# Three moves of work between queues in a one-core transformer-layer kernel: the first block's transposes, two weight sums, and the order inside half of a product

## The chip, the core and the metric

The kernel runs on one core of a Trainium2 chip. The core has five engines with queues of their own, each working strictly in order: TensorE (PE, with its weight loads shown as PEld), VectorE (DVE), ScalarE (ACT), GpSimd (POOL) and SyncE (SP, which only issues DMAs here). The metric is device time in microseconds, the median of several runs of the whole program, 721.55 us before the change (721.35 to 722.12).

## What is computed

One layer on 512 positions of 1024 channels, all in float32, batch 1:

```
u = rms_norm(h, g_mix);  z = u @ w_in              # 1024 -> 4360 columns
y_a = sliding_window_attention(q_a, k_a, v_a, sinks) @ w_br_swa    # 8 heads of 64
y_b = forgetting_attention(q_b, k_b, v_b, f_b + b_forget) @ w_br_fox
h = h + (gates[:, :, 0] * y_a + gates[:, :, 1] * y_b) @ w_mix_out
u = rms_norm(h, g_mlp)
h = h + square(relu(u @ w_ff1)) @ w_ff2            # 1024 -> 4096 -> 1024
h = h + sigmoid(rms_norm(h, g_ple) @ w_ple_gate) * (p @ w_ple_proj)
out = rms_norm(h, g_final)
```

Float32 accuracy is kept on PE by writing each operand as a high half and a low half (`hi_lo`, L68: ACT casts the value to `fp32r`, DVE subtracts that from the value) and by summing three products: high by high, high by low, low by high.

## The kernel before, in words

**Order.** PE and POOL run in the order in which the program is written. In two stretches ACT and DVE do so too: in the whole start (L477, SP as well there) and from L1332 to the end of the third step of the feed-forward part (`man`, closed at L1382). Everywhere else the build lays out the order of ACT, DVE and SP on its own.

**The start (L477 to L544).** Four blocks of 128 positions are normalized and multiplied with the 648 columns of `w_in` that give the values and the forget logits. `square1` (L429) sums the squares of a block, one half on ACT and one on DVE; `scale1` (L443) has POOL turn the sum into the factor `rs` (two small operations in `rms_rstd`, L356: `n_ms`, then `n_rs`), and DVE scales both halves. `to_uT` (L373) transposes a half block on PE in four instructions and splits the result in high and low. `split_v(k)` (L451) splits one of eight slices of the weights: `wv_h` on ACT, `wv_l` on DVE. `v_mm(tb, k)` (L458) is six matmuls. For block 0 the written order is:

```
scale1(0, square1(0)); split_v(0)
to_uT half 0; v_mm(0, 0); split_v(1); v_mm(0, 1); split_v(2); split_v(3)
to_uT half 1; v_mm(0, 2); v_mm(0, 3)
acc = square1(1); split_v(4); split_v(5); scale1(1, acc); v_mm(0, 4); v_mm(0, 5)
```

Half 0 holds k = 0 to 3 of the block, half 1 holds 4 to 7.

**The feed-forward part (L1348 on).** Both big products are done in a scheme of seven block products in place of eight (Winograd's form of Strassen's): a product of pieces 1 to 7, of which 1 and 2 take a quadrant of the weights as it is, 3 a single quadrant too, and 5, 6, 7 and 4 take sums of quadrants. The hidden 4096 columns come in four quarters of two groups each. A quarter is 28 steps, written out in `STEPS` (L46): a and b are the first product (`f1`) of the quarter's two groups, A and B the second (`s2`):

```
a1 b1 a2 a5 b5 b2 a6 b6 a7 a3 b7 b3 A1 a4 b4 B1 A2 A5 B5 B2 A6 B6 A3 A7 B7 B3 A4 B4
```

Each step has one unit of weights. In the profile the units are numbered: the first quarter's a1 is u53, b1 u54, a2 u55, a5 u56, b5 u57, b2 u58, a6 u59, b6 u60, a7 u61, a3 u62, b7 u63, b3 u64, A1 u65, a4 u66, b4 u67, B1 u68, A2 u69, A5 u70, B5 u71. `emit_split` (L301) splits a unit (ACT L324, DVE L325, into one of four buffers). `sum_source` (L276) prepares the sum of quadrants ahead of that, in place, so a sum waits until the quadrant's earlier value has been split. The sums of A5, A7, B5 and B7 are done by DVE (L296); all others by an accumulating DMA that POOL issues (L298). The sums of b6 and b7 are emitted right after the split of b5 (`advance`, L328), inside the hand-ordered stretch. A quadrant's place takes the next load from memory (`emit_dma`, L246, issued by SP in order) once its last reader is done.

`win_mm` (L898) is the first product's step, 24 matmuls; `win_out` (L914) takes the result out of its bank (ACT L921 copies it, DVE L925 adds to it), and the next step in the same bank waits for that. `ff1_act` (L1257) applies relu and square on ACT; `ff2_op` (L1272) makes the operands 5, 6, 7 and 3 of the second product from sums of these, and splits them in `o` high (ACT L70) and `o` low (DVE L71).

`s2_mm` (L1296) is the second product's step: for each of two blocks of 128 positions six matmuls, with `oh`, `ol` the operand's halves and `wh`, `wl` the weights'. The order of the six is (j = 0: `oh wh`, `oh wl`, `ol wh`; then the same for j = 1).

Of the kernel before, what the change touches and what calls it, by code (L numbers as in the profile page):

```python
# [14 lines left out]
P = 128  # L15
# [35 lines left out]
def layer_kernel(ctx: ExitStack, tc: tile.TileContext, x, p, g_mix, w_in, b_forget, swa_sinks,  # L51
# [224 lines left out]
    def sum_source(i):  # L276

        if i in sources or i >= len(order) or not isinstance(order[i][1][0], (list, dict)):  # L280
            return
        emit_dma(i)
        key, (rs, pn, _), _ = order[i]

        first = {5: 1, 6: 5, 4: 6}.get(pn)
        if (first and unit_of[key[:-1] + (first,)] >= look["n"]
                or pn == 7 and unit_of[key[:-1] + (5,)] not in sources
                or any(raws[r]["tile"] is None for r in raws_of(i))):
            return
        if pn in (1, 2, 3):  # L290
            q = quadrant(i, pn in (2, 3), pn == 3)
        else:
            q = quadrant(i, 0, pn == 7)
            other = quadrant(i, *{5: (0, 1), 7: (1, 1), 6: (1, 1), 4: (1, 0)}[pn])
            if key[0] == "s2" and pn in (5, 7):
                nc.vector.tensor_tensor(q, q, other, ALU.add)  # L296
            else:
                nc.gpsimd.dma_start(q, other, accum_op=ALU.add)  # L298
        sources[i] = q if key[0] == "s2" else q.rearrange("q k (j c) -> q k j c", c=P)
# [70 lines left out]
                                           ALU.mult)  # L370
        return xn

    def to_uT(xn, uh, ul, tb, trp, name, tg="tr", halves=(0, 1)):  # L373

        for half in halves:
            tr = trp.tile([P, 4, P], F32, tag=tg, bufs=3, name=f"{name}_tr{half}")
            for j in range(4):
                k = half * 4 + j
                nc.tensor.transpose(tr[:, j, :], xn[:, k * P:(k + 1) * P], ident)
            sl = (slice(None), slice(half * 4, half * 4 + 4), slice(tb * P, (tb + 1) * P))  # L380
            hi_lo(uh[sl], ul[sl], tr)

    def new_uT(name):
        t = up.tile([P, 2 * KT * S + SHIFT], F32R, tag="u", bufs=1, name=name)
# [92 lines left out]
    with tc.manual_schedule(engines={ET.Activation, ET.DVE, ET.SP}):  # L477
        load_x(0)
        load_wv(0)
        load_wv(2)  # L480
        load_x(1)
        load_wv(4)
        load_wv(6)
        load_x(2)
        load_x(3)
        bcast_row(bf_bc, b_forget[0])
        bcast_row(sink_bc, swa_sinks[0])


        warm = psA.tile([P, 4, P], F32, tag="tr", bufs=3, name="warm")  # L490

        def warm_up(n):
            for j in range(n):
                nc.tensor.transpose(warm[:, j % 4, :], ident, ident)
        warm_up(N_WARM[0])
        ps = psA.tile([P, KT], F32, tag="mm", bufs=2, name="g_colps")
        nc.tensor.transpose(ps, g_row, ident[0:KT, 0:KT])
        nc.vector.tensor_copy(g_col, ps)
        warm_up(N_WARM[1])
        gps = []  # L500
        for half in range(2):
            ps = psA.tile([P, S], F32, tag="sc", bufs=3, name=f"g_ps{half}")
            for j in range(4):
                k = half * 4 + j
                nc.tensor.transpose(ps[:, j * P:(j + 1) * P],
                                    g_col[:, k:k + 1].to_broadcast([P, P]), ident)
            gps.append(ps)
        warm_up(N_WARM[2])
        scale1(0, square1(0))
        split_v(0)  # L510
        to_uT(xn1[0], uh, ul, 0, psA, "n1_0", halves=(0,))
        v_mm(0, 0)
        for k in (1, 2, 3):
            split_v(k)
            if k == 1:
                v_mm(0, 1)
        to_uT(xn1[0], uh, ul, 0, psA, "n1_0", halves=(1,))
        v_mm(0, 2)
        v_mm(0, 3)
        acc = square1(1)  # L520
        split_v(4)
        split_v(5)
        scale1(1, acc)
        v_mm(0, 4)
        v_mm(0, 5)
        split_v(6)
        split_v(7)
        for half in range(2):
            nc.scalar.copy(g_bc[:, half * 512:half * 512 + 512], gps[half])
        to_uT(xn1[1], uh, ul, 1, psA, "n1_1")  # L530
        v_mm(0, 6)
        v_mm(0, 7)
        for tb in range(1, NT):
            if tb < NT - 1:
                acc = square1(tb + 1)
                scale1(tb + 1, acc)
            v_out(tb - 1)
            for k in range(KT):
                v_mm(tb, k)
                if k == 4 and tb < NT - 1:  # L540
                    to_uT(xn1[tb + 1], uh, ul, tb + 1, psA, f"n1_{tb + 1}")
            if tb == 2:
                unit("ka")
        v_out(NT - 1)  # L544
# [751 lines left out]
    def s2_mm(g, pn):  # L1296
# [5 lines left out]
        for i in range(2):  # L1302
# [1 line left out]
                bank[g // 2, "2" + bk, i] = mm_tile(f"s2_{g}{bk}{i}", tg)  # L1304
            ps = bank[g // 2, "2" + bk, i]
            ts_ = slice(i * P, i * P + P)
            for j in range(2):
                for n, (o, w) in enumerate(((oh, wh), (oh, wl), (ol, wh))):
                    nc.tensor.matmul(ps, o[:, j, ts_], w[:, j, :],  # L1309
                                     start=tg != "" and j == 0 and n == 0,  # L1310
                                     stop=j == 1 and n == 2, skip_group_check=True)

    def s2_out(fq, pn):

# [178 lines left out]
```

## Time and profile before

| what | us |
|---|---|
| median of the runs | 721.55 |
| the profiled execution's own time | 721.84 |
| its span, first to last instruction | 720.1 |
| mean granted clock of TensorE | 0.997 |
| start until block 1 is transposed | about 17 |
| feed-forward part, four quarters of 28 steps | about 354 to 664 |

The span is what the profile's clock shows from the first to the last instruction; the program's own time has 1.7 us around it. PE is busy 98% of the span, so what matters is where it is not, and which instruction of which engine ended that idle time: in the rows of the profile this stands in square brackets, `[idle before <-releaser]`. An engine's gap that nobody waits for costs nothing.

### The profile page before, as it was taken

The numbers are of one execution on the slowest core, as the hardware profiler recorded it, in microseconds if no ns is written. First come the engines' busy times: TensorE is split into PE (matmuls) and PEld (weight loads), VectorE is DVE, ScalarE is ACT, GpSimd is POOL, SyncE is SP. The second block draws the span as 40 slices with busy tenths as digits, with TensorE's granted clock in tenths as the row PEclk, the third lists the DMA queues.
The fourth block names the chain that finished last, engine by engine and source line by source line (L and its number), as shares of the span: only waits on it lengthen the run. The fifth ranks groups of instructions, "written<-read, shape, count | busy, mean of one in ns | idle before, by whom it ended". The sixth has DMA issues, their size and how long they took to land.

```text
span 720.1 us, 11455 instructions
## 1 busy us (share of the span) xinstructions
PE 705.6 (98%) x4229; PEld 626.6 (87%) x4229; DVE 531.5 (74%) x900; ACT 449.4 (62%) x836; POOL 87.6 (12%) x127
## 2 busy tenths in 40 slices
PE   7999999999999999999999999999999999999995
PEld 6988888888888998888899789988999889988884
DVE  5567888877696556545879985899679966997564
ACT  5547888779863553344777646874578546866452
POOL 1011211100001200002410102010300020010101
PEclk9999999999999999999999999999999999999998
DMA  9256456670364894450995598739994689079002
GB/s 290 65 155 159 109 136 154 150 197 1 118 206 116 152 339 162 160 173 11 252 220 202 105 285 168 235 87 254 190 259 113 157 234 227 31 147 349 1 30 87
DMA packets 74055, 116.72 MB, mean 162 GB/s; under 512 B 6664, under 2 KB 44048, under 8 KB 74000
## 3 DMA queue, kind: packets, MB, share of 16 engines
q1 hardware_dynamic: 65792, 86.38, 37.9%
q0 software_dynamic: 8064, 29.36, 22.2%
q8 instruction: 33, 0.54, 0.3%
q10 hardware_dynamic: 144, 0.26, 0.1%
q14 instruction: 22, 0.18, 0.1%
HBM read 72.93 MB, written 4.19 MB: 107 GB/s over the span
## 4 chain that ended last, share of the span: by engine, by line
PE 85%; DVE 9%; ACT 2%; issue 2%; DMA 1%; POOL 0%; POOLq 0%; DVEq 0%; ACTq 0%
PE pf L74 5%; PE pf L76 5%; PE pf L75 5%; PE s_6x L1309 3%; PE s_4x L1309 3%; PE s_0x L1309 3%; PE s_2x L1309 3%; PE h_sc L752 2%; PE h_pv L822 2%; PE h_tr L810 2%; PE psy L75 2%; PE psy L76 2%; PE psy L74 2%; PE psm L76 2%; PE psm L75 2%; PE psm L74 2%
## 5 line engine op out<-in xcount | busy, mean ns | idle before, releaser
L298 POOL DMA_DIRECT2D wq<-wq x26 | 23.6, 942 | 174.9 <-DVE u154l L325 25.9
L770 ACT ACTIVATE s<-s,h_nm 128x128 f32<-128x128 f32 (+1 forms) x64 | 32.6, 512 | 5.9 <-DVE h_nm L763 5.1
L359 POOL TENSOR_SCALAR n_ms<-acc 128x1 f32<-128x1 f32 x15 | 6.3, 419 | 164.8 <-ACT junk L1075 100.4
L71 DVE TENSOR_TENSOR h_ptl<-h_tr,h_pth 128x512 fp32r<-128x512 f32 (+2 forms) x40 | 22.9, 604 | 3.9 <-ACT h_pth L70 3.6
L467 PE MATMUL va<-wv_h,u 128*128 128x320 f32 x64 | 20.1, 319 | 0.8 <-ACT u L70 0.7
L70 ACT CAST h_pth<-h_tr 128x512 fp32r<-128x512 f32 (+2 forms) x40 | 19.4, 523 | 1.8 <-PE h_tr L810 1.4
L70 ACT CAST u<-n_tr 128x512 fp32r<-128x512 f32 x22 | 12.2, 586 | 13.1 <-PE n_tr L1123 5.9
L810 PE MATMUL h_tr<-ident,s 128*128 128x128 f32 x136 | 19.6, 277 | 0.2
L467 PE MATMUL vb<-wv_h,u 128*128 128x328 f32 x64 | 19.6, 313 | 0.0
L298 POOL DMA_DIRECT2D wgw<-wgw x8 | 7.1, 970 | 101.9 <-DVE u25l L325 77.7
L71 DVE TENSOR_TENSOR u<-n_tr,u 128x512 fp32r<-128x512 f32 x22 | 14.6, 685 | 6.5 <-ACT u L70 6.5
L1075 ACT ACTIVATE junk<-h_sb 128x512 f32<-128x512 f32 x16 | 10.1, 630 | 12.3 <-DVE h_sb L1065 9.8
L822 PE MATMUL h_pv<-h_pth,v 128*128 128x256 f32 (+1 forms) x64 | 17.3, 291 | 0.0
L822 PE MATMUL h_pv<-h_ptl,v 128*128 128x256 f32 (+1 forms) x64 | 16.9, 305 | 0.3 <-DVE h_ptl L71 0.3
L810 PEld LDWEIGHTS h_tr<-ident,s 128*128 128x128 f32 x136 | 15.0, 141 | 2.0 <-ACT s L790 0.5
L1399 DVE TENSOR_TENSOR sgp<-sgp,pp 128x512 f32<-128x512 f32 (+1 forms) x9 | 5.7, 633 | 14.6 <-ACT sgp L1398 14.6
L1065 DVE TENSOR_TENSOR h_sb<-psm,h_sb 128x512 f32<-128x512 f32 x8 | 5.5, 689 | 14.3 <-PE psm L76 14.3
L790 ACT ACTIVATE s<-s,h_rec 128x128 f32<-128x128 f32 (+2 forms) x32 | 14.2, 482 | 2.3 <-DVE h_rec L784 2.3
L832 DVE TENSOR_TENSOR h_ao<-h_pv,h_ao 64x512 f32<-64x512 f32 x16 | 10.9, 681 | 6.1 <-ACT h_ao L831 5.8
L758 DVE CUSTOM_DVE_ANT_0 s<-h_sc,causal 128x128 f32<-128x128 f32 (+3 forms) x32 | 13.8, 482 | 0.3 <-PE h_sc L752 0.3
L784 DVE RECIPROCAL h_rec<-h_den 128x4 f32<-128x4 f32 x16 | 3.0, 185 | 14.5 <-ACT s L770 14.3
L822 PEld LDWEIGHTS h_pv<-h_ptl,v 128*128 128x128 f32 x64 | 12.1, 188 | 1.7 <-DVE h_ptl L71 0.8
(1607 smaller groups left out, 2773.8 us busy)
## 6 DMA issues: line engine op xcount, KB each, us to landing
wq<-in_w_ff_dram SPq DMA_DIRECT2D x45, 512.0 KB, 5.7
wq<-wq POOLq DMA_DIRECT2D x26, 512.0 KB, 5.1
wq_c<-in_w_ff_dram SPq DMA_DIRECT2D x9, 512.0 KB, 5.8
wg<-in_w_in_dram SPq DMA_DIRECT2D x4, 1024.0 KB, 5.4
wgw<-in_w_in_dram SPq DMA_DIRECT2D x8, 512.0 KB, 5.2
wgw<-wgw POOLq DMA_DIRECT2D x8, 512.0 KB, 5.8
wmix<-in_w_mix_out_dram SPq DMA_DIRECT2D x4, 1024.0 KB, 4.9
wpg<-in_w_ple_gate_dram SPq DMA_DIRECT2D x4, 1024.0 KB, 8.6
```

The source lines that it names most:

```text
L70: nc.scalar.copy(hi, src)
L71: nc.vector.tensor_tensor(lo, src, hi.bitcast(F32), ALU.subtract)
L74: nc.tensor.matmul(ps, lh, rh, start=start, stop=False)
L75: nc.tensor.matmul(ps, lh, rl, start=False, stop=False)
L76: nc.tensor.matmul(ps, ll, rh, start=False, stop=stop)
L298: nc.gpsimd.dma_start(q, other, accum_op=ALU.add)
L467: nc.tensor.matmul(ps, u[:, kk_, ts_], w[:, kk_, c0:c1], start=kk_ == 0 and n == 0, stop=kk_ == KT - 1 and n == 2)
L752: nc.tensor.matmul(ps[:, off:off + n], qs[i][z][:, qb * P:(qb + 1) * P], kk[i][z][:, k0:k0 + n], start=z == 0, stop=z == 1)
L770: nc.scalar.activation(sl, sl, AF.Exp, bias=nm[:, qb:qb + 1], accum_out=den[:, qb:qb + 1])
L810: nc.tensor.transpose(tr[:, n, :], c["s"][:, o, :], ident)
L822: nc.tensor.matmul(pv[:, q0:q0 + nq, :], V2[kb][:, c["v"], :], t[:, o:o + nq, :], start=n == 0, stop=n == 2 * NT - 1, skip_group_check=True)
L1309: nc.tensor.matmul(ps, o[:, j, ts_], w[:, j, :], start=tg != "" and j == 0 and n == 0, stop=j == 1 and n == 2, skip_group_check=True)
```

## The change

1. In the start, `to_uT` is cut in two: `to_uT_pe` (the four transposes of a half) and `to_uT_split` (its high and low half). For block 0 both halves' transposes are written ahead of everything else of PE, the second half's split comes behind `split_v(2)`, and `square1(1)` moves up from behind `v_mm(0, 3)` to ahead of `split_v(3)`. `v_mm(0, 1)` to `v_mm(0, 3)` keep their order on PE.
2. The sums of b6 and b7 of the first quarter (`("f1", 1, 6)` and `("f1", 1, 7)`, u60 and u63) are done by DVE in place of POOL's accumulating DMAs. The other three quarters keep the DMAs.
3. In `s2_mm` the six matmuls run as `oh wh`, `oh wl` for j = 0, the same for j = 1, then `ol wh` for j = 0 and for j = 1. This holds for all 56 steps of the second product.

```diff
-            if key[0] == "s2" and pn in (5, 7):
+            if key[0] == "s2" and pn in (5, 7) or key in (("f1", 1, 6), ("f1", 1, 7)):
                 nc.vector.tensor_tensor(q, q, other, ALU.add)
             else:
                 nc.gpsimd.dma_start(q, other, accum_op=ALU.add)
...
-    def to_uT(xn, uh, ul, tb, trp, name, tg="tr", halves=(0, 1)):
-
-        for half in halves:
-            tr = trp.tile([P, 4, P], F32, tag=tg, bufs=3, name=f"{name}_tr{half}")
-            for j in range(4):
-                k = half * 4 + j
-                nc.tensor.transpose(tr[:, j, :], xn[:, k * P:(k + 1) * P], ident)
-            sl = (slice(None), slice(half * 4, half * 4 + 4), slice(tb * P, (tb + 1) * P))
-            hi_lo(uh[sl], ul[sl], tr)
+    def to_uT_pe(xn, trp, name, half, tg="tr"):
+
+        tr = trp.tile([P, 4, P], F32, tag=tg, bufs=3, name=f"{name}_tr{half}")
+        for j in range(4):
+            k = half * 4 + j
+            nc.tensor.transpose(tr[:, j, :], xn[:, k * P:(k + 1) * P], ident)
+        return tr
+
+    def to_uT_split(tr, uh, ul, tb, half):
+        sl = (slice(None), slice(half * 4, half * 4 + 4), slice(tb * P, (tb + 1) * P))
+        hi_lo(uh[sl], ul[sl], tr)
+
+    def to_uT(xn, uh, ul, tb, trp, name, tg="tr"):
+
+        for half in range(2):
+            to_uT_split(to_uT_pe(xn, trp, name, half, tg), uh, ul, tb, half)
...
         scale1(0, square1(0))
+        trs0 = [to_uT_pe(xn1[0], psA, "n1_0", half) for half in range(2)]
         split_v(0)
-        to_uT(xn1[0], uh, ul, 0, psA, "n1_0", halves=(0,))
+        to_uT_split(trs0[0], uh, ul, 0, 0)
+        split_v(1)
         v_mm(0, 0)
-        for k in (1, 2, 3):
-            split_v(k)
-            if k == 1:
-                v_mm(0, 1)
-        to_uT(xn1[0], uh, ul, 0, psA, "n1_0", halves=(1,))
+        v_mm(0, 1)
+        split_v(2)
+        to_uT_split(trs0[1], uh, ul, 0, 1)
+        acc = square1(1)
+        split_v(3)
         v_mm(0, 2)
         v_mm(0, 3)
-        acc = square1(1)
         split_v(4)
...
-            for j in range(2):
-                for n, (o, w) in enumerate(((oh, wh), (oh, wl), (ol, wh))):
-                    nc.tensor.matmul(ps, o[:, j, ts_], w[:, j, :],
-                                     start=tg != "" and j == 0 and n == 0,
-                                     stop=j == 1 and n == 2, skip_group_check=True)
+            terms = [(o[:, j, ts_], w[:, j, :]) for o, ws in ((oh, (wh, wl)), (ol, (wh,)))
+                     for j in range(2) for w in ws]
+            for n, (o, w) in enumerate(terms):
+                nc.tensor.matmul(ps, o, w, start=tg != "" and n == 0, stop=n == 5,
+                                 skip_group_check=True)
```

## The prediction

> **What bounds the kernel now.** I read the page first, then a table of stretches, then the list of waits, then the timeline where TensorE (PE) waits.
>
> ```profile
> span 720.1 us, 11455 instructions
> PE 705.6 (98%) x4229; PEld 626.6 (87%) x4229; DVE 531.5 (74%) x900; ACT 449.4 (62%) x836; POOL 87.6 (12%) x127
> ```
>
> PE is the bound: 705.6 of 720.1 us. What PE computes is not changed, so time can only come out of its 14.5 idle us and of gaps too short to be called idle. The columns below are stretch, its length, then the busy time of PE, PE's weight loads, DVE, ACT and POOL.
>
> ```profile
> 9.00:18.00 9.00, 7.93 (x49) 6.62 (x49) 7.71 (x13) 6.79 (x13) 2.01 (x2) 1.00 1.09 336
> 18.00:56.00 38.00, 38.00 (x232) 35.72 (x231) 23.19 (x67) 19.69 (x57) 5.09 (x11) 1.00 0.40 114
> 56.00:205.00 149.00, 148.44 (x821) 127.76 (x820) 115.64 (x349) 122.48 (x325) 13.22 (x22) 1.00 0.49 130
> 340.00:377.00 37.00, 36.29 (x261) 33.48 (x260) 28.16 (x32) 27.36 (x44) 13.31 (x14) 1.00 0.92 219
> 377.00:433.00 56.00, 55.31 (x317) 48.35 (x316) 51.00 (x63) 34.87 (x46) 5.16 (x6) 1.00 0.72 200
> 433.00:510.00 77.00, 76.86 (x505) 69.90 (x504) 63.34 (x75) 48.99 (x65) 10.40 (x12) 1.00 0.77 191
> ```
> ```profile
> PE s_0z L1309 <- DVE o L71: 0.7, 1, 0.7
> PE ('f1', 0)x L910 <- ACT u_('f1', 0)_4203 L921: 0.7, 1, 0.7
> PE h_pv L822 <- DVE h_ptl L71: 0.3, 1, 0.3
> ```
>
> PE loses 1.07 us in the start, 0.71 before 377, 0.69 in the first quarter of the feed-forward part, 0.14 in a later one. From 18 to 56 it loses nothing, so what the start gains is handed on. The list names what two of these losses wait for. The chain of work that ended last is in those stretches PE itself, and gives PE's pace:
>
> ```profile
> 379.66 2.72 PE ('f1', 0)z L910 x24
> 416.26 2.72 PE s_0z L1309 x12
> ```
>
> A product of either kind takes 2.72 us: 0.113 a matmul in the first (L910), 0.227 in the second (L1309).
>
> **The change, part by part.**
>
> *The start.* The second norm block's scaling at 16.04 decides: PE's transposes wait for it.
>
> ```profile
> 5.28 0.56 SPq L425 DMA_DIRECT2D wv<-in_w_in_dram  x1
> 8.83 2.00 ACT L453 CAST wv_h<-wv 128x648 fp32r<-128x648 f32 x3
> 9.60 2.32 DVE L454 TENSOR_TENSOR wv_l<-wv,wv_h 128x648 fp32r<-128x648 f32 x3
> 11.83 0.59 ACT L70 CAST u<-n_tr 128x512 fp32r<-128x512 f32 x1 [0.99 <-PE n_tr L379]
> 13.06 0.68 DVE L435 CUSTOM_DVE_ANT_0 n_xn<-x 128x512 f32<-128x512 f32 x1
> 13.69 1.58 DVE L454 TENSOR_TENSOR wv_l<-wv,wv_h 128x648 fp32r<-128x648 f32 x2
> 13.91 1.44 POOL L359 TENSOR_SCALAR n_ms<-acc 128x1 f32<-128x1 f32 x1 [7.09 <-DVE acc L435]
> 15.44 0.57 POOL L362 TENSOR_TENSOR n_rs<-n_ms,mhalf 128x1 f32<-128x1 f32 x1
> 16.04 1.41 DVE L447 SCALAR_TENSOR_TENSOR n_xn<-x,n_rs,g_ps 128x512 f32<-128x512 f32 x2 [0.77 <-POOL n_rs L362]
> 16.93 1.29 PE L379 MATMUL n_tr<-ident,n_xn 128*128 128x128 f32 x8 [0.60 <-DVE n_xn L447]
> 20.37 0.30 POOL L359 TENSOR_SCALAR n_ms<-acc 128x1 f32<-128x1 f32 x1 [4.36 <-ACT n_xn L439]
> ```
> ```profile
> wv<-in_w_in_dram SPq DMA_DIRECT2D x1, 520.0 KB, 6.9
> ```
>
> The second half's transposes move ahead of the first products, so ACT's cast at 11.83 no longer waits 0.99 for them. ACT runs `wv_h` for k=1 and 2 (0.63 apart, from 8.83), then that cast at about 10.1, then the square of block 1 at 10.6. DVE runs `wv_l` for k=1 and 2 (0.75 apart, from 9.60), the low half at 11.1, the square at 11.7 (before: 13.06) and `wv_l` 3 at 12.35. The sum of squares is there at 12.4, 1.35 us sooner. POOL can't use all of it. At 13.91 its `n_ms` took 1.44 us and ended 0.08 after the two `wv_l` beside it (13.69 + 1.58 = 15.27); at 20.37, with DVE idle, the same operation took 0.30. Now three `wv_l` follow the square. The raw data of k=4 land at 5.28 + 6.9 = 12.2, with a second, smaller piece that I put at 12.5 (an estimate, behind it by SP's spacing), so `wv_h` 4 ends near 13.3 and `wv_l` 4 and 5 run from 13.35 to 14.95. `n_ms` slips through the gap at 13.2; `n_rs` then meets `wv_l` 4 and 5. Held, `n_ms` kept 0.08 of its 0.30 to do, so some 0.2 can pass before the hold; by that `n_rs` (0.57) ends 0.35 to 0.4 behind them, near 15.35. If there is no gap, `n_ms` ends near 14.75 and `n_rs` at 15.4. Either way the scaling starts at 15.4: **0.64 us** gained. Bounds: if POOL never waits, DVE's own order (behind `wv_l` 5) gives 14.9 and a gain of 1.15; if it waits in full twice, 15.7 and 0.3. The price is on PE: the square now stands ahead of `wv_h` 3 on ACT and `wv_l` 3 on DVE, which is there at 13.2, while PE, having no transposes in between, wants it at about 12.4. From 13.2 PE has 16 matmuls left ahead of the transposes, at 49 instructions in 7.93 us 0.16 each: they end near 15.8. The transposes are due at 15.4 + 0.89 (16.93 - 16.04) = 16.3, so the stop is hidden, with 0.5 us to spare; without that cover it would cost 0.8. The transposes that move to the front run while ACT casts the first half, where PE has nothing else.
>
> On this point the Trainium skill ("SBUF — State Buffer", section "Who interferes with whom") says that a VectorE instruction with two SBUF inputs shuts out a GpSimd instruction that reads SBUF until it ends. The 1.44 beside 0.30 agrees. By that rule the start gains 0.64; if the 1.44 were chance, 1.15.
>
> *The two sums.* They are those of b's products 6 and 7 in the first quarter (u60, u63).
>
> ```profile
> 363.02 1.76 POOL L298 DMA_DIRECT2D wq<-wq  x2 [3.80 <-DVE u57l L325]
> 369.13 1.05 ACT L324 CAST u60h<-wq 128x1024 fp32r<-128x1024 f32 x1 [2.35 <-DMA wq<-wq]
> 370.22 1.22 DVE L325 TENSOR_TENSOR u60l<-wq,u60h 128x1024 fp32r<-128x1024 f32 x1 [2.71 <-ACT u60h L324]
> 371.74 0.85 POOL L298 DMA_DIRECT2D wq<-wq  x1 [4.99 <-DVE u60l L325]
> 375.70 0.28 PE L910 MATMUL ('f1', 1)x<-u,u60l 128*128 128x256 f32 x1
> 376.02 0.58 ACT L921 COPY u_('f1', 0)_4203<-('f1', 0)x 128x512 f32<-128x512 f32 x1
> 376.65 0.50 PE L910 MATMUL ('f1', 0)x<-at_ff,u61h 128*128 128x256 f32 x2 [0.68 <-ACT u_('f1', 0)_4203 L921]
> 385.95 1.23 DVE L296 TENSOR_TENSOR wq_gb<-wq_gb,wq 128x1024 f32<-128x1024 f32 x1 [0.46 <-DMA wq<-in_w_ff_dram]
> ```
>
> PE stops at 376.65 for a bank that ACT copies late (376.02), and ACT is late since it waited until 369.13 for the DMA sum issued at 363.02. PE was due at 375.70 + 0.11, so 0.84 is lost. The sums are emitted behind u57l, which released POOL shortly before 363.02. On DVE one takes 1.23 (the same shape at 385.95), so the first ends near 363.9 and the second, 1.14 later, near 365. They stand ahead of u58l, the addition of a's second product (L925) and u59l, each 2.3 later. PE's cover: it ended u60 at 375.81, so by 2.72 a product it began u58 at 367.65 and wanted u58l at its third matmul, 367.9; u58l now ends near 366.1, or 366.7 behind the addition: 1.2 to spare. For DVE itself the idle 2.71 at 370.22 covers the 2.3. POOL's next sum waits for u59l, 2.3 later, but its reader, u66, is seven products (19 us) behind u59. ACT's u60h needs the buffer that PE leaves with u56 (364.9): it can start at 365, or at 368 if it stays behind the activation, the copy and the cast that wait for the addition (365.6 + 2.3). Before it was 369.13, so the copy comes out 1.1 us or more sooner: the stop is gone. Behind it, u60l ends 1.3 to 2.6 sooner, so POOL's next sum (371.74) and the weight loads that wait in SP's queue for its landing come sooner too, and with them the load that DVE waits for at 385.95. If DVE's order puts u58l ahead of the addition as well, u60h starts at 368.9 and only 0.2 is gained. I take the stop as gone.
>
> *The order within the second product.*
>
> ```profile
> 404.43 0.39 PE L1309 MATMUL s_0z<-u71l,o 128*128 128x512 f32 x1
> 405.51 0.73 PE L1309 MATMUL s_0z<-u71h,o 128*128 128x512 f32 x2 [0.69 <-DVE o L71]
> 406.08 0.40 PE L1309 MATMUL s_0z<-u71l,o 128*128 128x512 f32 x1
> ```
> ```profile
> 482.16 0.39 PE L1309 MATMUL s_2z<-u99l,o 128*128 128x512 f32 x1
> 482.69 0.73 PE L1309 MATMUL s_2z<-u99h,o 128*128 128x512 f32 x2
> ```
> ```profile
> 636.53 0.39 PE L1309 MATMUL s_6z<-u155l,o 128*128 128x512 f32 x1
> 637.06 0.74 PE L1309 MATMUL s_6z<-u155h,o 128*128 128x512 f32 x2
> ```
>
> The third waits for the low half of `o`: 405.51 - 404.43 - 0.23 = 0.85 lost in the first quarter, 0.30 in each of three others (first and last shown). After a stop PE needs 0.11 more (405.51 to 406.08 for two, not 0.45). With the change the low half comes fifth, 2 x 0.227 = 0.45 later. In three quarters 0.30 < 0.45, and **3 x 0.41 = 1.23** goes. The number of matmuls and weight loads stays, and the low weights stay second, so nothing new is waited for. In the first quarter 0.85 - 0.45 = 0.40 is left, and PE arrives 0.95 sooner besides (0.84 + 0.11): DVE must be 1.35 us sooner there. It is busy without a break from 385.95 on; before that it follows PE (0.95 sooner) and then the load, where 0.46 of idle lies: 1.41 if the load comes in time. So the wait just goes: **0.95 + 0.96 = 1.91** for both stops of the first quarter. The bound from below, DVE's chain not moving at all, leaves 0.45 of the two.
>
> *Sum.* 0.64 + 1.91 + 1.23 = 3.8. The profiled execution took 721.84 (1.7 around its span); the median of the runs is 721.55. 721.55 - 3.8 = **717.8 us**.
>
> **The rivals.**
> 1. DVE's chain in the first quarter moves little (a late load at 385.95, or u60h kept behind the activation): the second stop grows by what the first gives back. 0.45 to 1.4 instead of 1.91; about 718.8. For it: 51.0 of 56.0 us of DVE are busy there.
> 2. POOL is never held in the start: gain 1.15, **717.3**. Against it: 1.44 beside 0.30.
> 3. The reordering brings nothing, because what waits is not the low half but the end of DVE's queue just behind it: 1.23 and the 0.45 are lost, 3.8 - 1.7 = 2.1 left, **719.4**. If rival 1 holds as well, within 0.2%. Against: the waits name `o` L71.
> 4. Slower: outside the start and its few hand-ordered steps, the order of ACT and DVE is laid out when the kernel is built, and a start some tenths sooner can lay it out otherwise in the attention stage (56 to 205). Price: one stop as at `h_pv`, 0.3 + 0.11. With sixteen heads it decides from ten such stops (ten make up for 3.8; thirteen make it slower by over 0.2%); all sixteen cost 6.6, **724.3**. Against: the list has one now, and PE is busy 148.44 of 149.00.
>
> **How the numbers follow.** Forecast 0.55, rival 1 0.20, rival 2 0.10, rival 3 0.09, slower 0.06. Range: 716.8 (rival 2 and a first quarter a little better) to 720.0 (start 0.3, first quarter 0.45, later 0.8). A measurement tells about 0.2% (1.4 us) from no change. Faster by more holds in all of the forecast, rival 2, most of rivals 1 and 3: 0.87; same 0.07; slower 0.06.
>
> **What would show it.** After: the second block's scaling at 15.4 with `n_ms` or `n_rs` ending just behind the `wv_l`; u60h near 366, no PE wait on the copy L921; no wait of `s_*z` on `o` L71 in any quarter; PE's start-up transposes near 16.3. It is wrong if u60h still stands at 369, if `s_0z` waits by more than before, or if attention shows more than two waits of `h_pv` or `h_tr`.

## The result, and the profile after

The changed kernel takes 717.4 us, the median of 4 runs (717.36 to 717.6); the kernel before took 721.58 beside it (721.35 to 722.12). The ratio is 0.9942 with a 95% interval of 0.993 to 0.9955: 4.2 us or 0.6% faster. Forecast were 717.8 in a range of 716.8 to 720.0. The profiled execution of the changed kernel took 717.6 with a span of 715.9, at a mean granted clock of 0.998.

The head of the page after, with span and busy times:

```profile
span 715.9 us, 11454 instructions
PE 704.2 (98%) x4229; PEld 626.8 (88%) x4229; DVE 533.6 (75%) x902; ACT 449.6 (63%) x836; POOL 85.2 (12%) x125
```

PE has as many instructions as before (4229), and its idle time went from 14.5 us to 11.7. The span shrank by 4.2, though, and the idle time by only 2.8: a matmul that nothing follows at once is counted busy for 0.39 where it takes the place of 0.227, so the first 0.16 of a stop, and the slower restart behind it, stand as busy time (705.6 before, 704.2 after). DVE has two instructions more and POOL two less: the two sums.

The table of stretches after; the columns are stretch, length, busy time of PE, PE's weight loads, DVE, ACT and POOL, then clock, DMA share and GB/s:

```profile
9.00:18.00 9.00, 8.25 (x51) 7.22 (x52) 8.56 (x15) 7.65 (x15) 1.31 (x2) 1.00 1.06 324
56.00:205.00 149.00, 148.44 (x821) 127.86 (x820) 116.07 (x349) 121.72 (x326) 13.23 (x22) 1.00 0.50 131
340.00:377.00 37.00, 36.97 (x272) 34.48 (x271) 30.90 (x34) 28.17 (x44) 11.29 (x12) 1.00 0.84 209
377.00:433.00 56.00, 56.00 (x325) 49.35 (x324) 51.15 (x63) 34.55 (x45) 5.85 (x8) 1.00 0.70 192
433.00:510.00 77.00, 77.00 (x509) 70.38 (x508) 63.51 (x74) 50.02 (x65) 10.60 (x14) 1.00 0.78 192
```

In the feed-forward part PE's idle time is gone: 0.69 in the first quarter's stretch and 0.14 in the next became 0. In the attention (56 to 205) PE has the same 821 instructions and the same 148.44 busy: nothing was laid out otherwise there.

Of the list of PE's waits before, the rows of the start, which are not shown above:

```profile
PE n_tr L379 <- DVE n_xn L447: 1.1, 2, 0.6
PE va L467 <- ACT u L70: 0.7, 1, 0.7
PE va L467 <- DVE wv_l L454: 0.3, 1, 0.3
```

The whole list after, without the wait for the constants at the very start:

```profile
PE va L474 <- DVE wv_l L461: 0.6, 1, 0.6
PE n_tr L378 <- DVE n_xn L454: 0.5, 1, 0.5
PE h_pv L830 <- DVE h_ptl L71: 0.3, 1, 0.3
```

The waits for `o` L71 and for the copy (L929 now) are gone. Of the two waits for `n_xn`, block 1's is gone; the 0.5 left is block 0's. The wait of the first products for ACT's `u` is gone from the list because the second half's transposes now fill it; those products begin at 8.99 as before. A wait for `wv_l` is still there: 0.3 for slice 4 before, 0.6 for slice 3 now. That is the price that the moved square was to have.

How much sooner PE begins a piece of work than before, from its timelines (first matmul of each):

| first matmul of | before | after | sooner by |
|---|---|---|---|
| block 1's transposes | 16.93 | 16.07 | 0.86 |
| the attention's scores | 58.05 | 57.07 | 0.97 |
| b6 (u60) | 373.09 | 372.09 | 1.00 |
| a7 (u61) | 376.65 | 374.81 | 1.84 |
| B5 (u71) | 404.20 | 402.24 | 1.97 |
| the unit behind it (u72) | 407.91 | 404.98 | 2.93 |
| second quarter's u100 | 485.09 | 481.73 | 3.36 |
| third quarter's u128 | 562.28 | 558.50 | 3.77 |
| fourth quarter's u156 | 639.50 | 635.27 | 4.23 |
| end of the span | 720.12 | 715.87 | 4.25 |

So 0.97 comes from the start, 0.97 from a7's stop (1.00 to 1.97), 0.96 from B5's (1.97 to 2.93), and 0.43, 0.41 and 0.46 from the three later quarters.

*The start after.* DVE's and POOL's timelines:

```profile
11.70 0.68 DVE L442 CUSTOM_DVE_ANT_0 n_xn<-x 128x512 f32<-128x512 f32 x1
12.30 0.83 DVE L461 TENSOR_TENSOR wv_l<-wv,wv_h 128x648 fp32r<-128x648 f32 x1
13.58 1.58 DVE L461 TENSOR_TENSOR wv_l<-wv,wv_h 128x648 fp32r<-128x648 f32 x2 [0.44 <-ACT wv_h L460]
15.07 1.40 DVE L454 SCALAR_TENSOR_TENSOR n_xn<-x,n_rs,g_ps 128x512 f32<-128x512 f32 x2
```
```profile
12.56 0.74 POOL L359 TENSOR_SCALAR n_ms<-acc 128x1 f32<-128x1 f32 x1 [5.74 <-DVE acc L442]
13.38 0.57 POOL L362 TENSOR_TENSOR n_rs<-n_ms,mhalf 128x1 f32<-128x1 f32 x1
```

The square runs at 11.70, as worked out. `n_ms` takes 0.74 and ends 0.17 behind `wv_l` 3 (12.30 + 0.83 = 13.13). `n_rs` begins in the gap, at 13.38, takes its plain 0.57 and is ready at 13.95, while DVE is busy with `wv_l` 4 and 5 until 15.15. The scaling carries no bracket: it waits for nothing but its turn on DVE. PE's timeline shows the other half:

```profile
13.19 0.42 PE L474 MATMUL va<-wv_l,u 128*128 128x320 f32 x1 [0.63 <-DVE wv_l L461]
...
14.46 0.42 PE L474 MATMUL va<-wv_l,u 128*128 128x320 f32 x1
...
15.92 0.32 PE L474 MATMUL vb<-wv_h,u 128*128 128x328 f32 x1
16.07 1.17 PE L378 MATMUL n_tr<-ident,n_xn 128*128 128x128 f32 x8
```

The transposes follow the matmul ahead of them without a stop: PE itself, held up at 13.19 and once more at 14.46, is now the last to be ready, by a tenth (the scaling alone would let the transposes start at 15.07 + 0.89 = 15.96, by the 0.89 between the two before). At 14.46 it waited for `wv_l` 4, which ended at 14.41; the matmul ahead started at 14.04, so 0.27 were lost beyond the usual 0.15, too little idle time to get a bracket.

*The first quarter after*, on DVE, ACT and POOL:

```profile
361.65 1.21 DVE L325 TENSOR_TENSOR u58l<-wq,u58h 128x1024 fp32r<-128x1024 f32 x1
362.79 2.35 DVE L296 TENSOR_TENSOR wq<-wq,wq 128x1024 f32<-128x1024 f32 x2
365.06 0.68 DVE L933 TENSOR_TENSOR u_('f1', 0)_3995<-('f1', 0)y,u_('f1', 0)_3995 128x512 f32<-128x512 f32 x1
...
383.43 1.22 DVE L296 TENSOR_TENSOR wq_gb<-wq_gb,wq 128x1024 f32<-128x1024 f32 x1
...
402.25 0.69 DVE L71 TENSOR_TENSOR o<-z_('f1', 1)_4130,o 128x512 fp32r<-128x512 f32 x1
```
```profile
364.09 1.05 ACT L324 CAST u60h<-wq 128x1024 fp32r<-128x1024 f32 x1 [1.60 <-PE ('f1', 0)z L918]
...
373.86 0.58 ACT L929 COPY u_('f1', 0)_4203<-('f1', 0)x 128x512 f32<-128x512 f32 x1
```
```profile
368.30 0.85 POOL L298 DMA_DIRECT2D wq<-wq  x1 [0.27 <-DVE u60l L325]
```

The two sums take 2.35 on DVE. u60h stands at 364.09 in place of 369.13, the copy at 373.86 in place of 376.02, and a7 starts at 374.81 behind a matmul of b6 with no bracket. The sum that POOL issued at 371.74 is issued at 368.30. The sum A7 on DVE, at 385.95 before with 0.46 of waiting for a load, is at 383.43 with none.

*The end.* What ends last in both programs isn't on the page's timeline; it is among the instructions of the kernel's last line (L1488 before, L1496 after). The columns are count, shortest, median and longest in ns, first and last start:

```profile
L1488 POOLq DRAIN  x3: 40/102/5266, 714.1 to 719.9; - x3
```
```profile
L1496 POOLq DRAIN  x3: 40/93/5102, 710.0 to 715.6; - x3
```

POOL's closing DRAIN begins beside POOL's last operation (714.07 and 714.11 before, 709.99 and 710.03 after) and ends 0.8 before the end of the span. It became 0.16 shorter. The last store does not end the program: SP's own closing DRAIN follows the store's landing by 0.5 and stands at 714.4 after, 0.7 ahead of the end of POOL's (715.1). PE's last matmul ends 4.08 sooner than before (711.60 to 707.52). That is 0.15 less than at u156, because in the last gate PE waits 0.04 for a weight (u168l) at 666.61 and pays the restart of 0.11; the shorter end brings the gain back to 4.25.

### The profile page after: what moved, and what is told of

The parts are those of the page before. It is cut to its first block, busy times and chain, and to the rows that moved or that the text cites. A ratio compares the mean times of both kernels' runs of the same rounds, so it can differ in the third digit from the quotient of the medians.

```text
span 715.9 us, 11454 instructions
## 1 busy us (share of the span) xinstructions
PE 704.2 (98%) x4229; PEld 626.8 (88%) x4229; DVE 533.6 (75%) x902; ACT 449.6 (63%) x836; POOL 85.2 (12%) x125
## 4 chain that ended last, share of the span: by engine, by line
PE 96%; DMA 2%; DVE 1%; ACT 0%; SPq 0%; issue 0%; POOLq 0%; DVEq 0%; POOL 0%; ACTq 0%
PE pf L74 5%; PE pf L76 5%; PE pf L75 5%; PE s_6x L1318 3%; PE s_4x L1318 3%; PE s_0x L1318 3%; PE s_2x L1318 3%; PE h_sc L760 3%; PE h_pv L830 2%; PE h_tr L818 2%; PE psm L76 2%; PE psm L75 2%; PE psy L75 2%; PE psy L76 2%; PE psm L74 2%; PE psy L74 2%
## 5 line engine op out<-in xcount | busy, mean ns | idle before, releaser
L298 POOL DMA_DIRECT2D wq<-wq x24 | 21.8, 936 | 166.7 <-DVE u98l L325 25.9
L71 DVE TENSOR_TENSOR h_ptl<-h_tr,h_pth 128x512 fp32r<-128x512 f32 (+2 forms) x40 | 22.9, 604 | 3.9 <-ACT h_pth L70 3.4
L71 DVE TENSOR_TENSOR u<-n_tr,u 128x512 fp32r<-128x512 f32 x22 | 14.6, 685 | 6.0 <-ACT u L70 6.0
L1407 DVE TENSOR_TENSOR sgp<-sgp,pp 128x512 f32<-128x512 f32 (+1 forms) x9 | 5.7, 633 | 14.5 <-ACT sgp L1406 14.5
L792 DVE RECIPROCAL h_rec<-h_den 128x4 f32<-128x4 f32 x16 | 3.0, 185 | 14.5 <-ACT s L778 14.3
```

Source lines behind the costliest of these rows:

```text
L71: nc.vector.tensor_tensor(lo, src, hi.bitcast(F32), ALU.subtract)
```

## The experiments

**Each part alone.** Each of these kernels has one of the three parts and the kernel before's code for the other two; they and `one_sum` ran beside one median of before, 721.32.

The start alone:

```diff
-            if ... or key in (("f1", 1, 6), ("f1", 1, 7)):
+            if key[0] == "s2" and pn in (5, 7):
...
-            terms = [... for o, ws in (...) for j in range(2) for w in ws]
+            terms = [... for j in range(2) for o, ws in (...) for w in ws]
```

> Only the new order of the start; the sums and the order within the second product as before. Theory (the stops are links of one PE chain and their gains add): block 1 is transposed at 16.07 instead of 16.93 as in the changed kernel, the shift stays 0.97 to the end, the stops at u61 and in the four quarters stay as before: 0.97 us faster, 720.6. Rival (something with a time of its own later, a load or DVE's chain in the first quarter, swallows the start's gain): under 0.3 us faster, and one of the later stops is longer than before.

Measured: 720.09 (719.59 to 720.92), ratio 0.998 [0.9971, 0.9989]: 1.23 faster, more than expected. Its profiled execution is the slowest of its eleven (720.92). In it block 1's scaling stands at 15.43 and PE is 0.62 sooner, not 0.97, because the square began only at 12.32 there. POOL's and DVE's rows:

```profile
13.18 0.74 POOL L359 TENSOR_SCALAR n_ms<-acc 128x1 f32<-128x1 f32 x1 [6.50 <-DVE acc L442]
14.01 1.19 POOL L362 TENSOR_TENSOR n_rs<-n_ms,mhalf 128x1 f32<-128x1 f32 x1
```
```profile
13.94 1.58 DVE L461 TENSOR_TENSOR wv_l<-wv,wv_h 128x648 fp32r<-128x648 f32 x2 [0.18 <-ACT wv_h L460]
15.43 1.40 DVE L454 SCALAR_TENSOR_TENSOR n_xn<-x,n_rs,g_ps 128x512 f32<-128x512 f32 x2
```

`n_rs` was held here: 1.19 in place of 0.57. It began inside `wv_l` 4 and ended at 15.20, 0.42 behind `wv_l` 4 but 0.32 ahead of `wv_l` 5's end (13.94 + 1.58 = 15.52). So it was held by one of the two, not by both, and the scaling still waited only for DVE's own order.

The theory also had the lead stay the same to the end, and that did not come. PE is 0.64 sooner at the attention's scores, 0.51 behind a7's stop, where ACT's copy came only 0.51 sooner (375.51), and 1.02 behind B5's: DVE no longer waited for the load ahead of A7's sum (384.89 in place of 385.95), the low half of `o` came 1.06 sooner (403.71), and the stop shrank from 0.85 to 0.30.

The two sums alone:

> Only the two sums on DVE; start and order as before. Theory: the stop at u61 goes (0.84 + 0.11), and DVE's chain behind it comes 1.5 us sooner, so the stop for the low half of o in the first quarter shrinks from 0.85 to about 0.2: 1.6 us faster, 720.0. Rival (DVE's chain in the first quarter has a time of its own): the stop at u61 goes, but the one in s_0z grows to 1.8; under 0.2 us faster.

Measured: 720.22 (720.06 to 720.49), ratio 0.9984 [0.9975, 0.9993]: 1.10 faster. The stop at a7 is gone, and of B5's the list of PE's waits keeps this:

```profile
PE s_0z L1317 <- DVE o L71: 0.2, 1, 0.2
```

From start to start that is 0.32 lost (404.06 - 403.51 - 0.23), without the restart, where about 0.2 was expected: the low half came 1.45 sooner (403.32) and PE 0.92, and 0.85 + 0.92 - 1.45 = 0.32. The later quarters lose 0.30 each, as before. The profile agrees with the expected 1.6 better than the median does: PE is 1.46 sooner behind B5.

The order of the six matmuls alone:

> Only the new order within the second product; start and sums as before. Theory: the low half is needed 0.45 us later, so the stops of 0.30 (with 0.11 of restart each) in three quarters go, and 0.85 in the first becomes 0.40: 3 x 0.41 + 0.45 = 1.7 us faster, 719.9. Rival (the instruction behind it on DVE's queue is late as well): the stops move to the next step, under 0.5 us faster.

Measured: 720.26 (719.66 to 721.09), ratio 0.9984 [0.9975, 0.9993]: 1.06 faster, against 1.7 expected. The later quarters lose nothing any more (PE gains 0.43, 0.39 and 0.45 there). The first keeps both stops in part:

```profile
PE ('f1', 0)x L917 <- ACT u_('f1', 0)_4203 L928: 0.4, 1, 0.4
PE s_0z L1317 <- DVE o L71: 0.4, 1, 0.4
```

At B5 0.54 is lost, not 0.40. In this execution the DMA sum landed sooner (u60h at 368.77 in place of 369.13), so a7's stop was 0.25 shorter without any edit to it, PE came to B5 0.36 sooner and the low half only 0.22: 0.40 + 0.36 - 0.22 = 0.54. Of PE's lead of 1.95 at u156, 0.44 is lost again in the gate behind the feed-forward part; the next run shows where.

What follows: by the medians the three parts alone are worth 1.23, 1.10 and 1.06, together 3.4, where 0.97, 1.6 and 1.7 were expected. The whole brought 4.2 in its own comparison and 3.9 and 3.8 in the two repeats further down. Each of these gains has an interval of 0.6 to 0.9 to either side, so the sum and the whole are not told apart. The traces do not say that one part needs another, either: of B5's stop of 0.85 the order alone takes 0.31 and the sums alone 0.53, which add up to 0.84. Only the restart of 0.11 goes with the last of it. In the profiles the three end 0.93, 1.51 and 1.51 sooner, together 3.95 of 4.25.

**One sum on DVE in place of two.** b7's sum goes back to POOL's DMA:

```diff
-            ... or key in (("f1", 1, 6), ("f1", 1, 7)):
+            ... or key == ("f1", 1, 6):
```

> The changed kernel, but only the sum of b6 is done by DVE; that of b7 is left to POOL's DMA. Theory (ACT stood idle for b6's sum alone; b7's is not wanted until u63, ten us later): same time as the changed kernel within 0.2 us, 717.4, with DVE 1.2 us less busy. Rival (a DMA sum of b7 holds up those of a4 and b4 and with them the loads that DVE waits for): the first quarter's stop in s_0z comes back, 0.3 us or more slower than the changed kernel.

Measured: 717.95 (717.34 to 718.39), ratio 0.9951 [0.9939, 0.9964]. The first quarter has no stop, and PE's times in the feed-forward part are those of the changed kernel to 0.1. What its profile loses against the changed kernel's stands behind u156: PE's lead over the kernel before is 4.29 there (changed kernel 4.23), 4.00 at the gate's first product (4.23) and 3.75 at PE's last matmul (4.08), and the DRAIN is 0.08 longer (5.18). The gate's first weights are cast by ACT when their load has landed, and the load sets the time; the changed kernel's row first:

```profile
656.25 0.72 ACT L315 ACTIVATE u165h<-wpg,g_ple_t 128x512 fp32r<-128x512 f32 x1 [1.63 <-DMA wpg<-in_w_ple_gate_dram]
656.58 0.72 ACT L315 ACTIVATE u165h<-wpg,g_ple_t 128x512 fp32r<-128x512 f32 x1 [2.01 <-DMA wpg<-in_w_ple_gate_dram]
```

That load was issued 0.06 sooner than in the changed kernel and landed 0.32 later. `all_sums` below, without any DMA sum of b7, loses as much in the gate (4.72, 4.46, 4.21), so b7's DMA is not the reason. It was b6's sum that caused the stop; b7's neither helps nor costs on PE's path up to u156.

**Is POOL held in the start?** Two kernels shift what POOL's small operations meet. In the first, `wv_l` 3 runs ahead of block 1's square, so that POOL meets `wv_l` 4 and 5:

```diff
-        acc = square1(1)
         split_v(3)
+        acc = square1(1)
```

> The changed kernel with wv_h and wv_l of k=3 ahead of block 1's square again (the transposes stay in front). The square then ends at 13.15 on DVE, and POOL's n_rs begins at 13.7, beside wv_l 4 and 5 (13.6 to 15.15). Theory (a DVE instruction with two SBUF inputs holds POOL's small operation until it ends): n_rs takes 1.5 us or more instead of 0.57 and ends behind wv_l 5, near 15.4; block 1's scaling starts at 15.45 instead of 15.07, and the kernel is about 0.4 us slower than the changed one, 717.8. Rival (POOL is not held; the 1.44 of n_ms before was chance): n_rs takes 0.57, the scaling stays at 15.07 behind wv_l 5, PE no longer waits for wv_l 3: same time or up to 0.3 us faster than the changed one.

Measured: 718.4 (718.27 to 718.89), ratio 0.9957 [0.9943, 0.997], 0.8 slower than the changed kernel beside it (717.57), where 0.4 was expected.

```profile
13.71 1.56 POOL L359 TENSOR_SCALAR n_ms<-acc 128x1 f32<-128x1 f32 x1 [6.90 <-ACT wv_h L460]
15.35 0.56 POOL L362 TENSOR_TENSOR n_rs<-n_ms,mhalf 128x1 f32<-128x1 f32 x1
```
```profile
13.61 1.58 DVE L461 TENSOR_TENSOR wv_l<-wv,wv_h 128x648 fp32r<-128x648 f32 x2
15.95 1.41 DVE L454 SCALAR_TENSOR_TENSOR n_xn<-x,n_rs,g_ps 128x512 f32<-128x512 f32 x2 [0.77 <-POOL n_rs L362]
```

`n_ms` began 0.11 behind the start of `wv_l` 4 and ended 0.08 behind `wv_l` 5 (15.19): 1.56 for an operation that takes 0.30 alone. DVE idled 0.77 for it, the scaling is back near its old place, and PE's transposes came 0.8 later than in the changed kernel. POOL is held, so the rival falls. The size was off because the one that was caught was `n_ms`, not `n_rs`: it was held through both `wv_l`, and the whole of `n_rs` still came behind it.

In the second, the raw slice k = 4 is loaded ahead of k = 5, so that `wv_l` 4 follows `wv_l` 3 without a gap:

```diff
-        nc.sync.dma_start(wv[:, :, 0:520], src[:, :, C_VB:C_VB + 520])
-        nc.sync.dma_start(wv[:, :, 520:648], src[:, :, C_VA:C_VA + 128])
+        for ks in (slice(0, 1), slice(1, 2)) if k == 4 else (slice(0, 2),):
+            nc.sync.dma_start(wv[:, ks, 0:520], src[:, ks, C_VB:C_VB + 520])
+            nc.sync.dma_start(wv[:, ks, 520:648], src[:, ks, C_VA:C_VA + 128])
```

> The changed kernel with the load of the raw weights of k=4 and 5 cut in two, k=4 first. Theory (after the change the start is set by the landing of k=4, which DVE's idle 0.44 ahead of wv_l 4 waits for): wv_h 4 starts some 0.4 us sooner, wv_l 4, wv_l 5 and block 1's scaling with it, unless POOL's n_rs is then held by wv_l 4; up to 0.4 us faster than the changed kernel, 717.0, or the same if n_rs is held. Rival (PE's own chain bounds the start already): scaling sooner, but transposes at 16.07 as before, same time.

Measured: 717.93 (717.76 to 718.58), ratio 0.9951 [0.9939, 0.9964]; no faster than the changed kernel beside it (717.57).

```profile
12.56 1.40 POOL L359 TENSOR_SCALAR n_ms<-acc 128x1 f32<-128x1 f32 x1 [5.75 <-ACT wv_h L461]
14.04 1.00 POOL L362 TENSOR_TENSOR n_rs<-n_ms,mhalf 128x1 f32<-128x1 f32 x1
```
```profile
12.30 2.32 DVE L462 TENSOR_TENSOR wv_l<-wv,wv_h 128x648 fp32r<-128x648 f32 x3
15.08 1.41 DVE L455 SCALAR_TENSOR_TENSOR n_xn<-x,n_rs,g_ps 128x512 f32<-128x512 f32 x2 [0.46 <-POOL n_rs L362]
```

DVE was through with its three `wv_l` at 14.62, half a microsecond sooner, and then waited 0.46 for POOL, so nothing was gained: with no gap on DVE, `n_ms` was held through `wv_l` 3 and 4, and `n_rs` through 5.

**The changed kernel again.** Since the start differs from execution to execution, it was run twice more.

> The changed kernel once more, on the chip of the other runs of this call, as their measure: 717.4, and in its profile no wait of s_0z, s_2z, s_4z or s_6z and none at u61.

> The changed kernel once more, as the yardstick for the run beside it: 717.4 +- 0.3 by the two results so far (717.4 and 717.57).

Measured: 717.57 (717.11 to 717.84), ratio 0.9943 [0.9931, 0.9956], and 717.58 (717.04 to 718.46), ratio 0.9945 [0.9931, 0.9959]. These are 3.9 and 3.8 below the kernel before beside them, and neither profile has a wait at u61 or on `o`. The result stands, a little smaller than 4.2, and the two starts are not alike. POOL's and DVE's rows of the first:

```profile
12.66 0.74 POOL L359 TENSOR_SCALAR n_ms<-acc 128x1 f32<-128x1 f32 x1 [5.84 <-DVE acc L442]
13.48 1.00 POOL L362 TENSOR_TENSOR n_rs<-n_ms,mhalf 128x1 f32<-128x1 f32 x1
```
```profile
12.40 2.40 DVE L461 TENSOR_TENSOR wv_l<-wv,wv_h 128x648 fp32r<-128x648 f32 x3
14.72 1.40 DVE L454 SCALAR_TENSOR_TENSOR n_xn<-x,n_rs,g_ps 128x512 f32<-128x512 f32 x2
```

Here DVE has almost no gap, `n_rs` is held by `wv_l` 4 only (it ends at 14.48), and DVE scales at 14.72. In the other execution `n_ms` took 1.40 and `n_rs` 1.00, as with the split load, and the scaling stood at 15.22 behind a wait of 0.46. Over the profiled executions, three with the old start and nine with the changed one:

| execution of | square | `n_ms` | `n_rs` | scaling | block 1's transposes |
|---|---|---|---|---|---|
| the kernel before | 13.06 | 1.44 | 0.57 | 16.04 | 16.93 |
| the two sums alone | 13.10 | 1.44 | 0.57 | 16.09 | 16.99 |
| the order alone | 13.06 | 1.44 | 0.56 | 16.04 | 16.93 |
| the changed kernel | 11.70 | 0.74 | 0.57 | 15.07 | 16.07 |
| the same, second | 11.79 | 0.74 | 1.00 | 14.72 | 15.78 |
| the same, third | 11.84 | 1.40 | 1.00 | 15.22 | 16.11 |
| start alone | 12.32 | 0.74 | 1.19 | 15.43 | 16.42 |
| one sum | 12.09 | 0.74 | 1.06 | 15.08 | 16.07 |
| all sums on DVE (next) | 11.69 | 0.74 | 1.03 | 14.65 | 15.67 |
| the same, second | 11.86 | 0.74 | 1.03 | 14.81 | 15.84 |
| twelve small transfers (below) | 11.96 | 0.74 | 1.24 | 15.13 | 16.12 |
| four small transfers | 11.78 | 0.74 | 1.02 | 14.72 | 15.77 |

The old start hardly varies, the changed one does: its transposes begin at 15.67 to 16.42, 16.0 in the mean, 0.9 to 1.0 sooner than with the old start. The profile with which the prediction is compared (0.86 there) is an ordinary one of them.

**The sums of b6 and b7 on DVE in all four quarters.**

```diff
-            ... or key in (("f1", 1, 6), ("f1", 1, 7)):
+            ... or key[0] == "f1" and key[1] % 2 and pn in (6, 7):
```

> The changed kernel with the sums of b6 and b7 on DVE in all four quarters, six more of 1.2 us. Theory (in the later quarters no one waits for these DMA sums, and DVE has 13 us idle per quarter there): same time as the changed kernel within 0.3 us. Rival (DVE is at its limit just before B5, where the low half of o now has only 0.15 us to spare): the stops in s_2z, s_4z and s_6z come back, 0.3 to 1.2 us slower.

> The same as all_sums (both sums on VectorE in all four quarters), which came to 716.99 where the changed kernel came to 717.57 in the same comparison, though no stretch of its profile was shorter by more than 0.1. Theory: the 0.6 was the spread of the start from execution to execution, and this comes within 0.3 of the changed kernel beside it, about 717.4. Rival: the later quarters hold a cost that the profiled execution did not show, and this is again 0.4 to 0.6 below the changed kernel, about 716.9.

Measured: 716.99 (716.75 to 717.35), ratio 0.9936 [0.9924, 0.9949], and 716.89 (716.56 to 718.06), ratio 0.9937 [0.9923, 0.9951]. Twice it is 0.6 to 0.7 below the changed kernel beside it (717.57 and 717.58). The first expectation missed on both sides: the time was not the same within 0.3, and the rival's stops at B5 did not come back. The second run's rival has the number right and the place wrong, for nothing differs in the later quarters: no stop of PE does. What differs stands behind the last store: SP issues it at 711.67 in a span of 715.2 (the second run), and at 711.87 in a span of 715.9 with the changed kernel. POOL's DRAIN in that run:

```profile
L1496 POOLq DRAIN  x3: 40/102/4612, 709.8 to 714.9; - x3
```

4.61 in place of 5.10. That is 0.5 of the gain; the rest is within the spread of the start. No more than 0.2 is left to win in this way: POOL's DRAIN ends at 714.4 there, and SP's, behind the landing of the last store, stands at 714.2.

**What the DRAIN depends on.** It is 5.27 long with 56 transfers on POOL's queue, 5.18 with 55, 5.10 with 54 and 4.61 with 48. The next two kernels add transfers of 512 bytes, into a tile that nobody reads, behind the attention: 12, then 4.

```diff
     hp = ctx.enter_context(tc.tile_pool(name="hp", bufs=1))
+    spare = hp.tile([P, 12], F32, name="spare")
+    for n in range(12):
+        nc.gpsimd.dma_start(spare[:, n:n + 1], mhalf)
```

> The changed kernel with 12 more transfers on GpSimd's software queue, of 512 bytes each, into a tile that nobody reads, issued behind the attention. In the profiles so far the time from the issue of the last store to the end of the span was 4.17 with 56 sums on that queue (before, 8064 packets), 4.0 with 54 (the changed kernel) and 3.51 with 48 (all_sums and all_sums_again), so about 0.08 for each transfer. Theory: the end of the program grows with the number of transfers on that queue, whatever their size; here it is 4.0 + 12 x 0.08 = 5.0, and the time 718.4, if the transfers delay nothing on their way. Rival: what shortened the end was the sums' place or their bytes, not the number; then the end stays at 4.0 and the time at 717.5.

Measured: 718.43 (717.88 to 718.57), ratio 0.9952 [0.9936, 0.9967], and for the wrong reason the time that was expected. The end is shorter, not longer, and the time was lost on the way: measured against the second execution of the changed kernel, PE loses 0.65 between the attention and the mixing stage, whose cause is open, and another 0.96 ahead of the gate, where ACT waits for the gate's first weights until 657.86 (655.76 there).

```profile
L1499 SPq DRAIN  x3: 7/7/7, 716.0 to 716.3; - x3
L1499 POOLq DRAIN  x3: 40/102/3714, 711.6 to 716.6; - x3
```

> The changed kernel with 4 instead of 12 of the 512 byte transfers on GpSimd's software queue (58 transfers in all; small_moves had 66). What ends last in the profiles is GpSimd's own closing instruction (a DRAIN at the kernel's last line): 5.27 us long with 56 transfers, 5.18 with 55, 5.10 with 54, 4.61 with 48, but 3.71 with the 66 of small_moves. Theory: it takes 0.083 for each transfer since the queue's ring was last gone through, whatever the size, and small_moves went past the ring's end; here the DRAIN is 5.10 + 4 x 0.083 = 5.43 long. Rival: it goes by bytes or by the sums, and is 5.10 again. A third outcome, under 5.0, would say that even the first few of these transfers free part of the ring. The time is not judged: the added transfers also shift the order around the attention's end.

Measured: one run, 718.5, with before at 721.6 (no interval; the time isn't judged here).

```profile
L1499 POOLq DRAIN  x3: 40/102/5429, 710.6 to 716.5; - x3
```

5.43, as worked out from the count: 0.082 for each transfer ((5.43 - 5.10) / 4, as (5.27 - 4.61) / 8), whether it moves 512 bytes or 512 KB. That the 66 transfers of `small_moves` gave 3.71 fits a ring that is gone through in between and leaves fewer to clear at the end; that part is argued from this one point and not shown. With 3.71 POOL's DRAIN ended at 715.3, ahead of SP's at 716.0, and the program ended 0.8 behind SP's: POOL's counts only as long as it ends later than the last store.

## Why the prediction was right, point by point

**What bounds.** Right. PE's work stayed (4229 instructions, 0.227 and 0.113 a matmul), and the gain came out of its stops, but for the end's 0.17, which makes up for the 0.15 lost in the last gate.

**The start: 0.64 forecast, 0.97 measured.** This is the mis-sized term of the sum. The square came at 11.70 and `wv_l` 3 at 12.30, as worked out. What failed is the step "`n_rs` then meets `wv_l` 4 and 5 ... ends 0.35 to 0.4 behind them". In the profiled execution `n_rs` began ahead of `wv_l` 4, because `wv_h` 4 waited for its data until 12.81 and the gap on DVE was 0.44, wider than I had put it; in others it did meet `wv_l` 4, but was held by that one alone and ended 0.42 behind it, in time. Only where DVE had no gap at all (the third execution, the split load) was POOL last, at 15.22 and 15.08. So the start was nearer to rival 2's 14.9 and 1.15 than to mine, though not for its reason: POOL is held in nearly every execution (1.00 to 1.24 for `n_rs`, 1.56 for `n_ms` with the square moved), just not for long enough. The whole time, 717.4, is nearer to rival 2's 717.3 than to the 717.8 as well; with its condition not met, that is luck of the number and nothing for that rival.

The Trainium skill ("SBUF — State Buffer", section "Who interferes with whom") says that a VectorE instruction with two SBUF inputs and a GpSimd instruction that reads SBUF contend for a shared port under an exclusive lock, and that the one that comes later waits for the whole of the other. The holds of 1.40 to 1.56 agree with it. Two details are beside it: `n_ms` is held through two instructions of DVE that follow without a gap, and ends 0.08 behind the second, while `n_rs` is held through one and ends 0.42 behind it. And where `n_rs` came first (13.38, `wv_l` 4 at 13.58, changed kernel), the later instruction did not wait: `wv_l` 4 took its usual 0.83. For that order, seen in this one execution, the measurement differs from the page and decides.

**The price on PE.** The wait for `wv_l` 3 was to cost 0.8 and to be hidden with 0.5 to spare. It cost 0.80 (13.19 - 12.24 - 0.15; the 0.63 in the bracket is only what is idle of it). What the prediction's 16 matmuls of 0.16 leave out is the second wait, 0.27 for `wv_l` 4 at 14.46. With the restart of 0.11 behind it, PE reaches the transposes at 16.07; without this second wait PE would have been there at 15.7, ahead of the scaling's 15.96, and the wait for `wv_l` 3 would have been hidden. Of the scaling's gain of 0.97, 0.86 are seen at the transposes' start and the rest behind it, where the restart after a stop (0.11) is saved.

**The two sums.** Right, and with more to spare. u60h was forecast near 366 and stands at 364.09: the build took it ahead of the activation and the copies. u58l, which I had put behind the two sums at 366.1, stands ahead of them at 361.65, so only the addition (365.06) and u59l pay for the 2.35. The copy comes 2.16 sooner, 1.16 of it beside PE's lead of 1.00 there, where 1.1 or more was forecast. a7's stop is gone: 0.97 where 0.95 was forecast.

**The order, first quarter.** Right. Needed were 1.35 sooner on DVE beside the start. The low half of `o` came 2.52 sooner (404.77 to 402.25), 1.55 of it beside the start's 0.97, with 0.2 to spare: it ends at 402.94, and the fifth matmul of B5 starts at 402.24 + 4 x 0.227 = 403.15. The third, at 402.69, would have waited, which is the 0.32 of the sums alone. The same 2.52 stands at the sum whose load I named (385.95 to 383.43).

**The order, later quarters.** 0.43, 0.41 and 0.46, together 1.30, where 3 x 0.41 = 1.23 was forecast.

**The rivals.** Rival 1 didn't come: DVE's chain moved enough. Rival 3 fell by the order alone. Rival 4 fell by the table: PE's 56 to 205 holds the same waits, and ACT, DVE, POOL and SP keep their order there. What no step had is the end's DRAIN, 0.17 of the 4.25.

## What to carry to other kernels

Where one engine is busy 98% of the time, add up its stops one by one, and for each find the operation that releases it and how much sooner that must come; two stops in a row in one stage can need two edits, and either alone leaves part of them. A stop that is shorter than two matmuls goes by reading the late operand two matmuls later, without any faster work. Small operations on GpSimd beside back-to-back VectorE instructions with two operands in SBUF took about two to five times what they took alone here, so look at where such an operation begins, and not at its plain length.

## What the runs showed of the hardware that was not expected

- The end of the program waits for GpSimd's closing DRAIN, which takes 0.082 us more for each transfer that GpSimd has issued, whatever its size (5.10 with 54, 5.43 with four more of 512 bytes, 4.61 with 48). In 13 of the 14 profiles the span ends 0.78 behind that DRAIN; in the one with 66 transfers it ends behind the last store. Moving six more sums to VectorE, where they cost PE nothing, made 716.9 to 717.0 of 717.6, 0.5 of it in this way; that is the best of the versions run. With 66 transfers the same instruction took 3.71, and why is open.
- GpSimd's 0.30 operation on 128 x 1 values took 0.74, 1.40, 1.44 or 1.56, and its 0.57 one 1.00 to 1.24, depending on which VectorE instruction it began beside, and on gaps of a few hundredths between those.
- The same start gave the scaling at 14.72, 15.07 and 15.22 in three executions of one kernel, a spread of 0.50, which is more than what was argued about (0.64 against 0.97). A stage that begins with loads is judged by several executions, not by one.
